# One chain of small operations for the norms of two token tiles

## The chip, the cores and the metric

One Trainium2 chip, one core of it. The metric is the device time of one execution in microseconds (us). The kernel before took 2983.17 us, the median of three runs (2980.04 to 2984.09). Each engine works through its own queue in order: PE (TensorE, products and transposes), PEld (loads of PE's stationary operand), DVE (VectorE), ACT (ScalarE), POOL (GpSimd) and SP (which issues the DMAs). An instruction that waits holds up all that stands behind it in its queue.

## The reference

Two layers over 512 latent and 256 context tokens of width 1024. A layer is a SwiGLU feed-forward (FFN1), a token mixing with three groups of heads (grouped-query attention, a long convolution, attention over compressed keys) and a second feed-forward (FFN2). Each of the three adds its gated result to the stream and norms the sum; before each stands a second norm with a scale and shift that depend on the conditioning:

```python
def layer_norm(x, g=None, b=None):
    xf = x.astype(jnp.float32)
    mu = jnp.mean(xf, -1, keepdims=True)
    var = jnp.mean(jnp.square(xf - mu), -1, keepdims=True)
    y = (xf - mu) * lax.rsqrt(var + EPS)
    ...
def rms_norm(x, g):
    xf = x.astype(jnp.float32)
    y = xf * lax.rsqrt(jnp.mean(jnp.square(xf), -1, keepdims=True) + EPS) * g
    ...
```

Inside the mixing, the query and key heads (width 64), the compressed queries (256) and the compressed keys (128) have the root-mean-square norm. So nearly everything that enters a product went through a reciprocal root just before.

## The kernel before

**Tiles.** Tokens lie on partitions in six tiles of 128: tiles 0 to 3 are latents, 4 and 5 context. `P[j]` is the stream of tile j. Each float32 factor is split into two float32r parts, and each product is three matmuls (`mm3`). `H` and `Hl` (in the rows Hhi, Hlo) hold the normed and modulated stream, transposed, for all tokens.

**The order.** All operations are first recorded. A list schedule (`Recorder.order`) then takes, for each engine, of what is ready the operation that stands first in the program; its table of costs and latencies sets the order in each queue, and so do the slots of the pools (22 units of 128x1024, 13 weight tiles, 12 small tiles, 8 PSUM banks): a tile takes a slot when an earlier one gives it back. All instructions are issued from line 295, so rows of the profile are told apart by tiles: p is PSUM, w a split weight, raw a weight as loaded, s a small tile, t a scratch unit, u a unit that lives longer.

**A norm.** `norm_stats` takes two `bn_stats` and one `bn_aggr` of a tile on DVE, adds EPS, makes the reciprocal root by `rsqrt` (a guess from the exponent's bits, then two polynomial steps; nine DVE operations of one column) and multiplies by minus the mean: 11 operations of one column for each tile. `norm` then applies it on ACT. `post` multiplies the sums by the gate (DVE), adds them to `P[j]` (POOL), norms `P[j]` and applies the gain on POOL and the bias on DVE. `pre` norms `P[j]` again, transposes it on PE, modulates it on ACT and writes H and Hl: PE starts the next stage with these transposes, and what they read (a scratch unit, t) is ACT's.

**The seams.** A feed-forward sums its 22 units of hidden columns in four parts. In the last one, `ffn` forms the down products of tiles 0, 1, 2 and 3 one after the other, each tile's two halves of 512 columns with six units in each (18 matmuls a half), and then of tiles 4 and 5 together, unit by unit in turns; after each tile come its `post` and the next stage's `pre`. `mix_out` does the same after the mixing with pairs of tiles, but with `post` and `pre` for each tile by itself. In the text a seam is the place where one stage's last sums end and the next one's first products begin: FFN1 to mixing at 606 to 683 us (layer 0) and 2203 to 2278 (layer 1), FFN2 to the next FFN1 at 1622 to 1690, mixing to FFN2 of layer 1 at 2577 to 2614.

**The mixing's norms.** `proj` multiplies H by a group of columns of the input weights, for one tile after the other, and calls `use` on each: `use_kv` norms two key heads (a chain of two columns) and the compressed keys (one column), `use_cq` the compressed queries (one column), `use_q` six query heads (six columns). The stretches 683 to 780 and 2278 to 2345 us hold most of this.

**Counts.** There are 82 chains of one column: 60 of layer norms and 22 of root-mean-square norms. There are also 12 of two columns for the key heads, 10 of six columns for the query heads, and three on pairs of input tiles at the start.

Of the kernel before, what the change touches and what calls it, by code (L numbers as in the profile page):

```python
# [24 lines left out]
SEQ = 512  # L25
# [24 lines left out]
class Recorder:  # L50
    """Takes down engine operations instead of issuing them, finds which must follow which, and issues them
    in the order of a list schedule: each engine takes, of what is ready, what stands first in the program.

    Tiles that share slots are handed them in program order, which keeps the schedule free of deadlocks.
    """

# [86 lines left out]
    def cost(eng, method, args, kw):  # L143
        """About how long (ns) the engine is held."""
# [34 lines left out]
    def order(self):  # L179
# [8 lines left out]
        # slots: the tiles of each tag in the order of their first use  # L188
# [9 lines left out]
        # a tile may take a slot before its turn where the program's order from there on still has its own  # L198
# [99 lines left out]
def weave(main, n, side, m):  # L298
    """Runs through both, main's n steps and side's m in proportion."""
    done = 0  # L300
    for i, _ in enumerate(main, 1):
        while done * n < i * m and done < m:
            next(side, None)
            done += 1
    for _ in side:
        pass


class _Slots:
    """The slots of a tag: when each falls free, and which tiles (by rank) have theirs."""  # L310
# [41 lines left out]
class Core:  # L352
    """The network's passes over one core's engines; tiles are 128 tokens, latents first."""
# [46 lines left out]
    def copy(self, out, in_):  # L400
        """A copy on whichever of the two engines is next in turn."""
# [7 lines left out]
    def weights(self, src, n, units=False):  # L409
        """Loads [128, n] of weights and splits them exactly into two float32r parts."""  # L410
# [9 lines left out]
    def mm3(self, out, sh, sl, mh, ml, first, last):  # L420
        """out (+)= s.T @ m with s = sh + sl, m = mh + ml."""
# [5 lines left out]
    def split(self, hi, lo, src, scale=None):  # L427
        """hi + lo = src (times a per-partition scale), both float32r; src may be in PSUM."""
# [9 lines left out]
    def rsqrt(self, y, v, t):  # L438
        """y = v ** -0.5 on small float32 tiles (t: scratch of the same shape)."""
        ts, tt = self.nc.vector.tensor_scalar, self.nc.vector.tensor_tensor  # L440
        stt = self.nc.vector.scalar_tensor_tensor
        one = v.shape[-1] == 1

        def vyy(t):
            if one:
                stt(t, v, y, y, ALU.mult, ALU.mult)
            else:
                tt(t, v, y, ALU.mult)
                tt(t, t, y, ALU.mult)

# [9 lines left out]
        if one:  # L460
            ts(p, p, t, 1.875, ALU.mult, ALU.add)
        else:
            tt(p, p, t, ALU.mult)
            ts(p, p, 1.875, None, ALU.add)
        tt(y, y, p, ALU.mult)

    def norm_stats(self, x):
        """(rstd, -mean * rstd, mean) of the rows of x [128, 1024]."""
        nc = self.nc
        st = self.small(24)  # L470
        for i, c in enumerate(HALVES):
            nc.vector.bn_stats(st[:, 6 * i:6 * i + 6], x[:, c])
        nc.vector.bn_aggr(st[:, 12:14], st[:, 0:12])
        r = self.small(4)
        nc.vector.tensor_scalar(r[:, 0:1], st[:, 13:14], EPS, None, ALU.add)
        self.rsqrt(r[:, 1:2], r[:, 0:1], r[:, 2:3])
        nc.vector.scalar_tensor_tensor(r[:, 3:4], st[:, 12:13], -1.0, r[:, 1:2], ALU.mult, ALU.mult)
        return r[:, 1:2], r[:, 3:4], st[:, 12:13]

# [1 line left out]
    def norm(self, x, out):  # L481
        """out = (x - mean) / deviation, row by row."""
        rstd, nmr, _ = self.norm_stats(x)
        for c in HALVES:
            self.nc.scalar.activation(out[:, c], x[:, c], AF.Identity, bias=nmr, scale=rstd)
        return out

    def norms(self, xs):
        """Norms the rows of several tiles in place, by one chain of small operations."""
# [14 lines left out]
        for j, x in enumerate(xs):  # L504
            for c in HALVES:
                nc.scalar.activation(x[:, c], x[:, c], AF.Identity, bias=nmr[:, j:j + 1], scale=y[:, j:j + 1])
        return xs

    def pre(self, l, j, x, kind):
        """H[:, :, tile j] = layer_norm(x) * (1 + scale) + shift."""  # L510
        nc = self.nc
        hn = self.norm(x, self.tmp())
        h = self.tmp()
        i = 0 if j < NLT else 1
        sh, sc = self.mcol[l][kind], self.mcol[l][kind + 1]
        for k0, c in zip((0, 4), HALVES):
            p = self.ps()
            for k in range(4):
                nc.tensor.transpose(p[:, 128 * k:128 * k + 128], hn[:, c][:, 128 * k:128 * k + 128], self.ident)
            for k in range(4):  # L520
                src, dst = p[:, 128 * k:128 * k + 128], h[:, c][:, 128 * k:128 * k + 128]
                b, m = sh[:, k0 + k, i:i + 1], sc[:, k0 + k, i:i + 1]
                nc.scalar.activation(dst, src, AF.Identity, bias=b, scale=m)
            hk = h[:, c].rearrange("p (k t) -> p k t", k=4)
            hi = self.H[:, k0:k0 + 4, 128 * j:128 * j + 128]
            nc.scalar.copy(hi, hk)
            nc.gpsimd.tensor_tensor(self.Hl[:, k0:k0 + 4, 128 * j:128 * j + 128], hk, hi.bitcast(F32), ALU.subtract)

    def post(self, j, P, acc, gate, gb, quick=False):
        """P = layer_norm(P + gate * acc, g, b); acc: pairs of a first column and the sums from there on."""  # L530
        nc = self.nc
        t = self.tmp()
        add = (nc.vector if quick else nc.gpsimd).tensor_tensor
        for c0, p in acc:
            c = slice(c0, c0 + p.shape[-1])
# [1058 lines left out]
```

## Time and profile before

| | |
|---|---|
| median of three runs | 2983.17 us |
| span of the profiled execution | 2980.4 us (no other time is given for that execution) |
| PE busy | 2850.9 us, 96% |
| DVE busy | 1781.7 us, 60% |
| ACT busy | 1057.1 us, 35% |
| POOL busy | 718.6 us, 24% |
| PE's idle time put down to ACT's scratch units t | 46.5 us in 26 waits |

A row of a stretch gives its length, then each engine's busy time (with the count of instructions), then PEclk, the mean clock that was granted to TensorE as a share of full speed. A row of the waits says what PE waited for: the engine and tile that came last, the us in total, how many times, and the longest. In rows of operations, out<-in are the tiles, then partitions x elements.

### The profile page before, as it was taken

Reading aid. Unit: us, or ns where it says so; the run is one execution under the profiler, and the core shown is the slowest. Engines: PE = TensorE matmul, PEld = TensorE weight load, DVE = VectorE, ACT = ScalarE, POOL = GpSimd, SP = SyncE. Lnnn points to the kernel's source line nnn. Section 1 sums busy time; section 2 is a strip of 40 time slices with the busy share of each in tenths; the row PEclk is TensorE's granted clock in tenths of the full one; section 3 lists DMA queues with packets and bytes.
Section 4 is the critical chain, followed back from the end, with each engine's and each line's share of the span. In section 5 each row is a group of like instructions: output and inputs, shape, how many; then the busy total and the mean of one; then the engine's idle time right before and its main releaser. Section 6 shows DMA issues by size and latency. Waiting matters only on the chain. (4 is left out here: it accounts for less than half of the span.)

```text
span 2980.4 us, 42000 instructions
## 1 busy us (share of the span) xinstructions
PE 2850.9 (96%) x16132; PEld 2431.1 (82%) x16132; DVE 1781.7 (60%) x4039; ACT 1057.1 (35%) x2050; POOL 718.6 (24%) x659
## 2 busy tenths in 40 slices
PE   7999999989999999999999999999998999899997
PEld 5888888868787789888887788888878777688886
DVE  6875757688667682757575744132268767723335
ACT  4212221255655653121222621211236647442221
POOL 2201223265011052013223410122145220310222
PEclk9999999989999999999999999999999999899999
DMA  7653434321021312434341231212122112123331
GB/s 262 230 159 117 138 124 137 110 100 52 30 70 39 107 44 71 148 121 150 109 149 46 96 119 57 78 51 70 71 84 71 41 50 93 57 92 106 99 107 56
DMA packets 105721, 291.42 MB, mean 98 GB/s; under 512 B 15184, under 2 KB 17392, under 8 KB 105520
## 3 DMA queue, kind: packets, MB, share of 16 engines
q1 hardware_dynamic: 105520, 288.73, 29.3%
q8 instruction: 127, 2.08, 0.3%
q14 instruction: 74, 0.61, 0.1%
HBM read 277.23 MB, written 11.45 MB: 97 GB/s over the span
## 5 line engine op out<-in xcount | busy, mean ns | idle before, releaser
L295 PE MATMUL p<-Hhi,w 128*128 128x256 f32 (+1 forms) x5536 | 1368.5, 337 | 8.0 <-DVE w L295 4.1
L295 PEld LDWEIGHTS p<-Hhi,w 128*128 128x128 f32 x5536 | 954.4, 191 | 121.9 <-DVE w L295 5.3
L295 PE MATMUL p<-Hlo,w 128*128 128x256 f32 (+1 forms) x2768 | 930.5, 337 | 0.0
L295 PE MATMUL p<-w,u 128*128 128x512 f32 x2904 | 671.6, 392 | 0.0
L295 DVE TENSOR_TENSOR w<-raw,w 128x1024 fp32r<-128x1024 f32 (+2 forms) x312 | 393.7, 1262 | 410.9 <-PE p L295 334.6
L295 PEld LDWEIGHTS p<-w,u 128*128 128x128 f32 x2904 | 546.1, 189 | 112.2
L295 ACT CAST w<-raw 128x1024 fp32r<-128x1024 f32 (+2 forms) x312 | 322.3, 1041 | 711.7 <-PE p L295 596.2
L295 PEld LDWEIGHTS p<-Hlo,w 128*128 128x128 f32 x2768 | 527.0, 190 | 54.5 <-POOL Hlo L295 1.2
L295 POOL TENSOR_TENSOR u<-t,u 128x512 fp32r<-128x512 f32 (+1 forms) x154 | 184.2, 1196 | 1246.2 <-ACT u L295 1170.8
L295 POOL TENSOR_TENSOR u<-u,t 128x512 f32<-128x512 f32 (+2 forms) x180 | 231.6, 1308 | 592.7 <-DVE t L295 367.1
L295 PE MATMUL p<-u,u 128*64 128x128 f32 (+7 forms) x2120 | 293.7, 326 | 22.2 <-DVE u L295 6.2
L295 DVE TENSOR_TENSOR t<-t,p 128x512 f32<-128x512 f32 (+1 forms) x160 | 90.6, 567 | 364.0 <-PE p L295 320.8
L295 PEld LDWEIGHTS p<-u,u 128*64 128x64 f32 (+4 forms) x2120 | 211.2, 160 | 84.0 <-issue 36.1
L295 DVE SCALAR_TENSOR_TENSOR junk<-adaw,crow 128x512 bf16<-128x512 f32 x256 | 201.4, 787 | 88.5 <-PE p L295 55.5
L295 ACT CAST u<-t 128x512 fp32r<-128x512 f32 (+1 forms) x154 | 81.3, 528 | 414.7 <-DVE t L295 407.2
L295 DVE SCALAR_TENSOR_TENSOR adaw<-adaw,crow 128x512 f32<-128x512 f32 x256 | 209.0, 816 | 6.1
L295 PE MATMUL p<-w,Hhi 128*128 128x416 f32 (+3 forms) x712 | 194.6, 356 | 7.9 <-DVE w L295 4.3
L295 DVE TENSOR_TENSOR t<-p,u 128x512 f32<-128x512 f32 x196 | 130.6, 684 | 100.3 <-PE p L295 99.5
L295 ACT ACTIVATE t<-p 128x512 f32<-128x512 f32 (+2 forms) x162 | 79.8, 496 | 273.8 <-PE p L295 273.7
L295 PE MATMUL p<-ident,t 128*128 128x128 f32 x848 | 124.8, 285 | 47.2 <-ACT t L295 42.2
L295 PEld LDWEIGHTS p<-ident,t 128*128 128x128 f32 x848 | 99.4, 145 | 69.9 <-ACT t L295 51.0
L295 PEld LDWEIGHTS p<-w,Hhi 128*128 128x128 f32 x712 | 131.2, 194 | 20.1 <-DVE w L295 9.0
(124 smaller groups left out, 2434.1 us busy)
## 6 DMA issues: line engine op xcount, KB each, us to landing
raw<-in_ffn_gu SPq DMA_DIRECT2D x176, 512.0 KB, 3.6
adaw<-in_ada_t SPq DMA_DIRECT2D x256, 256.0 KB, 2.8
raw<-in_ffn_down SPq DMA_DIRECT2D x88, 512.0 KB, 3.8
raw<-in_w_out_u SPq DMA_DIRECT2D x16, 512.0 KB, 3.3
u<-in_x_all SPq DMA_DIRECT2D x12, 512.0 KB, 7.6
xs<-u SPq DMA_DIRECT2D x12, 512.0 KB, 2.6
raw<-in_w_hy SPq DMA_DIRECT2D x12, 512.0 KB, 3.4
u<-grow SPq DMA_DIRECT2D x10, 512.0 KB, 5.1
```

Source lines behind the costliest of these rows:

```text
L295: getattr(getattr(self.nc, eng), method)(*args, **kw)
```

## The change

`rsqrt` is written in one way for any width, in ten operations. `stats` makes one chain of twelve for all tiles that it is given, each tile one column; `norms`, `pre` and `post` take lists of tiles. The last part of a feed-forward takes tiles in pairs (0, 1), (2, 3), (4, 5), each tile's two halves fully before the next tile's, then `post` and `pre` of both; the last feed-forward of all keeps single tiles (`step=1`). `mix_out` hands its pairs to `post` and `pre` as pairs. In the mixing, `proj` first takes the squares of a pair of tiles into one small tile (`take`) and then norms both (`use`): six columns for the key heads and compressed keys of two tiles, two for the compressed queries, twelve for the query heads. Comments are dropped, so line numbers stay. Built, the kernel has 606 fewer DVE instructions, 578 of them with a scalar operand and 28 TENSOR_TENSOR; the counts of PE, ACT, POOL and SP are the same.

```diff
     def rsqrt(self, y, v, t):
...
         ts(yi, yi, -1.0, 1595932665.0, ALU.mult, ALU.add)
-        vyy(t)
-        ts(t, t, -1.0, 2.38924456, ALU.mult, ALU.add)
-        stt(y, y, 0.703952253, t, ALU.mult, ALU.mult)
-        vyy(t)
+        tt(t, v, y, ALU.mult)
+        stt(t, t, -0.703952253, y, ALU.mult, ALU.mult)
+        stt(y, t, 1.68191409, y, ALU.add, ALU.mult)
+        tt(t, v, y, ALU.mult)
+        tt(t, t, y, ALU.mult)
         p = self.small(v.shape[-1])
         ts(p, t, 0.375, -1.25, ALU.mult, ALU.add)
-        if one:
-            ts(p, p, t, 1.875, ALU.mult, ALU.add)
-        else:
-            tt(p, p, t, ALU.mult)
-            ts(p, p, 1.875, None, ALU.add)
-        tt(y, y, p, ALU.mult)
...
+        tt(p, p, t, ALU.mult)
+        stt(y, p, 1.875, y, ALU.add, ALU.mult)
+
+    def stats(self, xs):
...
-    def post(self, j, P, acc, gate, gb, quick=False):
+    def post(self, Ps, accs, gates, gb, quick=False):
...
-        self.norm(P, P)
-        for c in HALVES:
-            nc.gpsimd.tensor_tensor(P[:, c], P[:, c], gb[0][:, c], ALU.mult)
-            nc.vector.tensor_tensor(P[:, c], P[:, c], gb[1][:, c], ALU.add)
+        self.norms(Ps)
+        for P in Ps:
+            for c in HALVES:
+                nc.gpsimd.tensor_tensor(P[:, c], P[:, c], gb[0][:, c], ALU.mult)
+                nc.vector.tensor_tensor(P[:, c], P[:, c], gb[1][:, c], ALU.add)
...
-                for js in [[j] for j in range(NLT)] + [[*range(NLT, ntok)]]:
-                    ps = {j: [] for j in js}
-                    for h in range(2):
-                        for j in js:
-                            ps[j].append((512 * h, self.ps()))
-                        for f in range(n):
-                            for j in js:
-                                down(ps[j][h][1], j, h, f)
+                for j0 in range(0, ntok, step):
+                    js = range(j0, j0 + step)
+                    ps = []
                     for j in js:
-                        self.post(j, P[j], ps[j], gate[j // NLT], gb, quick=j == tail)
-                        yield j
+                        ps.append([(512 * h, self.ps()) for h in range(2)])
+                        for h in range(2):
+                            for f in range(n):
+                                down(ps[-1][h][1], j, h, f)
+                    self.post([P[j] for j in js], ps, [gate[j // NLT] for j in js], gb, quick=j0 + step == tail)
+                    yield js
...
         def run(toks):
-            for j in toks:
+            toks = [*toks]
+            for q, j in enumerate(toks):
                 p = self.ps()[:, :n]
...
-                use(j, p)
+                take(j, p)
+                if (q + 1) % step == 0:
+                    use(toks[q + 1 - step:q + 1])
```

PE's queue before, at the end of FFN1 of layer 0 (row 3056 on): p_868 and p_869 are sums of tiles 4 and 5, t_822 is tile 0 after the norm of the mixing's `pre`.

```order
L295 MATMUL p_827<-ident_83,t_822 128x128 x4
L295 MATMUL p_869<-w_805,u_743 128x512
L295 MATMUL p_869<-w_806,u_743 128x512
L295 MATMUL p_869<-w_805,u_743 128x512
L295 MATMUL p_868<-w_805,u_743 128x512
L295 MATMUL p_828<-ident_83,t_822 128x128 x4
L295 MATMUL p_868<-w_806,u_743 128x512
```

The same place now (row 3072 on): p_866 is a sum of tile 5, t_827 and t_828 are tiles 0 and 1 after that norm.

```order
L295 MATMUL p_866<-w_799,u_707 128x512 x2
L295 MATMUL p_835<-ident_83,t_827 128x128 x4
L295 MATMUL p_866<-w_800,u_707 128x512
L295 MATMUL p_866<-w_799,u_707 128x512
L295 MATMUL p_838<-ident_83,t_828 128x128 x4
L295 MATMUL p_866<-w_805,u_743 128x512
L295 MATMUL p_836<-ident_83,t_827 128x128 x4
L295 MATMUL p_866<-w_806,u_743 128x512
L295 MATMUL p_839<-ident_83,t_828 128x128 x4
```

The transposes of tiles 0 and 1 have moved together, and from the interleaved sums of tiles 4 and 5 to those of tile 5, with tile 4's already behind them.

SP's queue before, at the same seam (row 281 on): xs_142 is the stream's copy in DRAM, u_283 and u_284 are tiles 0 and 1 of the stream, the raw tiles are the mixing's first weights.

```order
L295 DMA xs_142<-u_283 128x1024
L295 DMA adaw_2081<-in_ada_t 128x512
L295 DMA t_896<-in_ropeA 128x512
L295 DMA raw_933<-in_w_kv 128x832
L295 DMA xs_142<-u_284 128x1024
L295 DMA u_911<-in_hy_w 64x512
L295 DMA raw_936<-in_w_kv 128x832
L295 DMA raw_939<-in_w_kv 128x832
```

SP's queue now (row 283 on), with the same names for the stream.

```order
L295 DMA xs_142<-u_283 128x1024
L295 DMA xs_142<-u_284 128x1024
L295 DMA u_905<-in_hy_w 64x512
L295 DMA raw_927<-in_w_kv 128x832
L295 DMA u_906<-hdn 64x256
L295 DMA t_909<-in_hy_decay 128x256
L295 DMA raw_930<-in_w_kv 128x832
L295 DMA raw_933<-in_w_kv 128x832
```

The second of the four key and value weights was issued between the two stores; it now stands behind both.

## Rows read from the trace of the kernel before

**Rows 1.** Of the page's first part: busy us, share, instructions
```profile
PE 2850.9 (96%) x16132; PEld 2431.1 (82%) x16132; DVE 1781.7 (60%) x4039; ACT 1057.1 (35%) x2050; POOL 718.6 (24%) x659
```

**Rows 2.** Busy time by stretch; columns as the first line says
```profile
core 0: us, PE busy (x) PEld busy (x) DVE busy (x) ACT busy (x) POOL busy (x), PEclk, DMA share, GB/s
606.00:683.00 77.00, 62.33 (x317) 52.23 (x316) 63.14 (x175) 49.33 (x104) 47.80 (x37) 0.89 0.26 86
683.00:780.00 97.00, 84.27 (x504) 74.32 (x504) 81.96 (x362) 53.45 (x136) 32.72 (x72) 0.93 0.16 52
1622.00:1690.00 68.00, 57.80 (x346) 48.45 (x346) 58.62 (x161) 47.08 (x90) 38.26 (x29) 0.97 0.21 59
2203.00:2278.00 75.00, 64.24 (x346) 56.86 (x346) 68.82 (x209) 47.29 (x97) 49.94 (x56) 0.93 0.22 77
2278.00:2345.00 67.00, 58.41 (x289) 50.56 (x288) 57.79 (x235) 37.04 (x87) 30.41 (x49) 0.92 0.22 74
2577.00:2614.00 37.00, 23.06 (x142) 20.47 (x141) 32.51 (x95) 21.55 (x44) 18.24 (x13) 0.77 0.07 29
```

**Rows 3.** Waits of TensorE, 606 to 683: us in total, times, longest
```profile
PE p L295 <- ACT t L295: 10.3, 3, 6.4
PE p L295 <- DVE s L295: 3.1, 1, 3.1
```

**Rows 4.** Waits of TensorE, 683 to 780
```profile
PE p L295 <- DVE t L295: 4.0, 2, 2.0
PE p L295 <- DVE u L295: 2.4, 5, 0.9
```

**Rows 5.** Waits of TensorE, 1622 to 1690
```profile
PE p L295 <- ACT t L295: 10.2, 5, 3.5
```

**Rows 6.** Waits of TensorE, 2203 to 2278
```profile
PE p L295 <- ACT t L295: 6.9, 5, 4.2
```

**Rows 7.** Waits of TensorE, 2278 to 2345
```profile
PE p L295 <- DVE w L295: 4.1, 3, 3.3
```

**Rows 8.** Timeline of TensorE: start, us, operation, idle before it and its releaser
```profile
613.29 1.12 PE L295 MATMUL p<-ident,t 128*128 128x128 f32 x4 [6.35 <-ACT t L295]
```

**Rows 9.** VectorE's one-column operations: busy us, mean ns, idle before
```profile
L295 DVE SCALAR_TENSOR_TENSOR s<-s 128x1 f32<-128x1 f32 x180 | 70.4, 397 | 1.8
L295 DVE SCALAR_TENSOR_TENSOR s<-s,s 128x1 f32<-128x1 f32 x126 | 39.0, 317 | 0.8
L295 DVE TENSOR_SCALAR s<-s 128x1 f32<-128x1 f32 x246 | 34.0, 146 | 3.4 <-ACT t L295 1.5
L295 DVE TENSOR_TENSOR s<-s,s 128x1 f32<-128x1 f32 x82 | 24.5, 299 | 0.8
L295 DVE TENSOR_SCALAR s<-s 128x1 int32<-128x1 int32 x164 | 23.0, 146 | 1.2
L295 DVE TENSOR_SCALAR s<-s,s 128x1 f32<-128x1 f32 x82 | 16.7, 204 | 0.7
```

**Rows 10.** VectorE's two-column operations, same columns
```profile
L295 DVE TENSOR_TENSOR s<-s 128x2 f32<-128x2 f32 x108 | 16.7, 158 | 43.0 <-ACT t L295 42.0
L295 DVE TENSOR_TENSOR s<-s,s 128x2 f32<-128x2 f32 x78 | 15.5, 209 | 0.3
L295 DVE TENSOR_SCALAR s<-s 128x2 f32<-128x2 f32 x60 | 13.0, 227 | 0.3
L295 DVE SCALAR_TENSOR_TENSOR s<-s,s 128x2 f32<-128x2 f32 x15 | 2.5, 165 | 0.1
```

**Rows 11.** VectorE from 603 to 655 alone, same columns
```profile
L295 DVE SCALAR_TENSOR_TENSOR s<-s 128x1 f32<-128x1 f32 x24 | 10.2, 440 | 0.0
L295 DVE TENSOR_TENSOR w<-raw,w 128x832 fp32r<-128x832 f32 x4 | 4.1, 1014 | 2.0 <-PE p L295 2.0
L295 DVE TENSOR_SCALAR s<-s 128x1 f32<-128x1 f32 x24 | 3.2, 146 | 0.0
```

**Rows 12.** DMA issues: count, KB each, median us to landing
```profile
raw<-in_ffn_gu SPq DMA_DIRECT2D x176, 512.0 KB, 3.6
```

More of the change, by code (lines that the diff above doesn't have):

```diff
@@ L503, in norms @@
         nc.vector.scalar_tensor_tensor(nmr, mean, -1.0, y, ALU.mult, ALU.mult)
-        for j, x in enumerate(xs):
+        return [[x[:, j:j + 1] for x in (y, nmr, mean)] for j in range(n)]
+    def norms(self, xs, outs=None):
+        outs = outs or xs
+        for x, out, (rstd, nmr, _) in zip(xs, outs, self.stats(xs)):
             for c in HALVES:
-                nc.scalar.activation(x[:, c], x[:, c], AF.Identity, bias=nmr[:, j:j + 1], scale=y[:, j:j + 1])
-        return xs
-    def pre(self, l, j, x, kind):
+                self.nc.scalar.activation(out[:, c], x[:, c], AF.Identity, bias=nmr, scale=rstd)
+        return outs
@@ L511, in pre @@
+    def pre(self, l, js, xs, kind):
         nc = self.nc
-        hn = self.norm(x, self.tmp())
-        h = self.tmp()
-        i = 0 if j < NLT else 1
         sh, sc = self.mcol[l][kind], self.mcol[l][kind + 1]
[L516 to L527, printed above, removed]
@@ L529, in post @@
-    def post(self, j, P, acc, gate, gb, quick=False):
+        for j, hn in zip(js, self.norms(xs, [self.tmp() for _ in xs])):
+            h = self.tmp()
+            i = 0 if j < NLT else 1
+            for k0, c in zip((0, 4), HALVES):
+                p = self.ps()
+                for k in range(4):
+                    nc.tensor.transpose(p[:, 128 * k:128 * k + 128], hn[:, c][:, 128 * k:128 * k + 128], self.ident)
+                for k in range(4):
+                    src, dst = p[:, 128 * k:128 * k + 128], h[:, c][:, 128 * k:128 * k + 128]
+                    b, m = sh[:, k0 + k, i:i + 1], sc[:, k0 + k, i:i + 1]
+                    nc.scalar.activation(dst, src, AF.Identity, bias=b, scale=m)
+                hk = h[:, c].rearrange("p (k t) -> p k t", k=4)
+                hi = self.H[:, k0:k0 + 4, 128 * j:128 * j + 128]
+                nc.scalar.copy(hi, hk)
+                nc.gpsimd.tensor_tensor(self.Hl[:, k0:k0 + 4, 128 * j:128 * j + 128], hk, hi.bitcast(F32), ALU.subtract)
@@ L544, in post @@
[L544 to L547 removed]
+        for P, acc, gate in zip(Ps, accs, gates):
+            t = self.tmp()
+            for c0, p in acc:
+                c = slice(c0, c0 + p.shape[-1])
+                nc.vector.tensor_tensor(t[:, c], p, gate[:, c], ALU.mult)
+                add(P[:, c], P[:, c], t[:, c], ALU.add)
+        if quick:
+            for P, (rstd, _, mean) in zip(Ps, self.stats(Ps)):
+                for c in HALVES:
+                    nc.vector.scalar_tensor_tensor(P[:, c], P[:, c], mean, gb[0][:, c], ALU.subtract, ALU.mult)
+                    nc.vector.scalar_tensor_tensor(P[:, c], P[:, c], rstd, gb[1][:, c], ALU.mult, ALU.add)
+            return
@@ new lines, in mix, with take_kv @@
+        kvt, kvn = {}, {}
+        kvs = [None]
+        def take_kv(j, p):
+            t = kvt[j] = self.unit()
+            nc.scalar.copy(t[:, 512:928], p)
+            if j % 2 == 0:
+                kvs[0] = self.small(6)
+            i, p = j % 2, t[:, 512:928]
+            kn = kvn[j] = self.tmp()
+            self.head_squares(p[:, 0:128], 2, kvs[0][:, 2 * i:2 * i + 2])
+            nc.scalar.activation(kn[:, 256:384], p[:, 256:384], AF.Square, accum_out=kvs[0][:, 4 + i:5 + i])
+            nc.gpsimd.tensor_copy(Vj(j, 0, 128), p[:, 128:256])
@@ L1472, in run @@
             n = NLT if last else NT
-            for j, P in self.mix_out(l, n):
-                self.pre(l, j, P[j], 6)
+            for js, P in self.mix_out(l, n):
+                self.pre(l, js, [P[j] for j in js], 6)
             fill = (x for k in range(0, 0 if last else 6) for x in self.ada(l + 1, k))
-            for j in self.ffn(l, 2, n, P, fill, tail=n - 1 if last else None, first=FIRST[l]):
+            for js in self.ffn(l, 2, n, P, fill, tail=n if last else None, first=FIRST[l], step=1 if last else 2):
                 if last:
-                    for c in HALVES:
-                        self.load(self.out[128 * j:128 * j + 128, c], P[j][:, c])
+                    for j in js:
+                        for c in HALVES:
+                            self.load(self.out[128 * j:128 * j + 128, c], P[j][:, c])
                 else:
-                    self.pre(l + 1, j, P[j], 0)
+                    self.pre(l + 1, js, [P[j] for j in js], 0)
 @with_exitstack
```

180 lines of the change are left out of this document (78 added, 102 removed).

## The prediction, made before the changed kernel ran

> **What bounds the kernel now.** I read the page's busy shares first. PE works 2850.9 us of the 2980.4 us span, 96% [rows 1]: at most 129.5 us can be won without giving PE less work or a higher clock, and the change leaves PE's work as it is. So DVE's saving counts only where PE stands still and the last thing to come was behind DVE's chains.
>
> Next come the stretches [rows 2]. Idle time of PE is length less busy: 14.7 us in 606 to 683, 12.7 in 683 to 780, 10.2 in 1622 to 1690, 10.8 in 2203 to 2278, 8.6 in 2278 to 2345, 13.9 in 2577 to 2614; together 70.9, more than half of all idle time. DVE is busy 82 to 92% there, against 60% over the span [rows 1, 2].
>
> Then the waits of each stretch say what came last. In 606 to 683 it is ACT's scratch t (10.3 us) and a small tile of DVE (3.1) [rows 3]; in 683 to 780 DVE's t and u, 4.0 and 2.4 [rows 4]; in 1622 to 1690 t, 10.2 [rows 5]; in 2203 to 2278 t, 6.9 [rows 6]; in 2278 to 2345 a weight split on DVE, 4.1 [rows 7]. ACT's t is what `norm` writes, after the chain on DVE: ACT is named because it came last, yet it had room, 49.33 of 77 us [rows 2]. The clearest instance is at 613.29 us: the transposes of tile 0 waited 6.35 us for t [rows 8].
>
> **What the change takes from DVE.** A chain of one column costs 70.4 + 39.0 + 34.0 + 24.5 + 23.0 + 16.7 = 207.6 us over 82 chains, 2.53 us each (eleven operations for a layer norm) [rows 9]. A pair's chain has 4 TENSOR_SCALAR, 4 TENSOR_TENSOR and 4 SCALAR_TENSOR_TENSOR of two columns. By their rows it is 4 x 0.227 + 3 x 0.158 + 0.209 + 4 x 0.165 = 2.25 us [rows 10], for two tiles. Of the 60 layer norms by single tiles 56 become 28 pairs: 56 x 2.53 - 28 x 2.25 = 78.7 us less. These drop 56 x 11 - 28 x 12 = 280 instructions. The kernel loses 606; four last chains gain one each, so some 330 go with the mixing's norms. At the mean of the one-column rows, 207.6 us over 880 instructions or 0.236, they are 78 us. DVE goes from 1782 to about 1625 us, 9% less.
>
> No row shows an operation of twelve columns or one on a strided six. The bounds are 0.158 us (a TENSOR_TENSOR of two columns) and 0.397 (a SCALAR_TENSOR_TENSOR of one) [rows 9, 10]; I take the lower half, since a column more made nothing dearer than 0.227 there. The ends differ by 55 operations x 0.24 = 13 us of DVE, spread over two layers, and the range holds that.
>
> **What reaches PE, seam by seam.** Three things come into the way of a full gain. A pair's chain can't begin before the second tile's sums: tile 0 now waits 36 matmuls more, 36 x 62.33/317 = 7.1 us [rows 2]. Behind the waiting statistics stand, in DVE's queue, operations of the next pair, but the schedule puts ready work ahead of them. Second, the work that was next latest is still there: ACT, POOL and the weight splits, which share the queues. Third, what PE had as filler moves too. In 606 to 683 PE reaches the first transposes 25 matmuls later than before (4.9 us by the same pitch), between the sums of tile 5. All four sets stand together there, where tile 1's stood 30 matmuls behind tile 0's.
>
> Nothing in the rows tells how the wait divides between the chains and what is next. The bounds are nothing and all of the wait. I take half, and name what takes the other half.
>
> - 606 to 683: (10.3 + 3.1) / 2 = 6.7 us [rows 3]. Next late: the mixing's weight splits, 1.01 us each on DVE [rows 11], now issued together. The clock comes to this: the stretch had 0.89 of full clock, 1622 to 1690 with like work 0.97 [rows 2], so 0.08 x 77 = 6.2 us is lost to it. With half the stall gone I take half of that too, 3.1.
> - 683 to 780: (4.0 + 2.4) / 2 = 3.2 [rows 4]. Next late: POOL's rotary products, whose count is unchanged.
> - 1622 to 1690: 10.2 / 2 = 5.1 [rows 5]. Next late: ACT, busy 47.08 of 68 us [rows 2].
> - 2203 to 2278: 6.9 / 2 = 3.5 [rows 6]. Next late: POOL's low parts and the splits, as in layer 0.
> - 2278 to 2345: 4.1 / 2 = 2.1 [rows 7]. The split waits in DVE's queue among the small operations that go.
> - 2577 to 2614: nothing. The pair is ready about when tile 1 was, so tile 0 comes later and tile 1 no sooner; PE's 13.9 us idle and its 0.77 of clock [rows 2] stay. All or a third of it either way are the bounds, -4.6 to +4.6.
> - The end: four single chains with one operation more, 0.165 to 0.227 us each [rows 10], of which the last tile's counts: +0.3 us with its issue.
> - The other norms of `mix_out` in layer 0 and the pairs at the start lie beside products that run on; ±1.
>
> Sum: 6.7 + 3.1 + 3.2 + 5.1 + 3.5 + 2.1 - 0.3 = 23.4 us. The profiled span becomes 2980.4 - 23.4 = 2957.0. The median of the runs shown is 2.8 us above that span, so the time is 2959.8, say 2960 us.
>
> **A rule against it.** In 603 to 655 us a SCALAR_TENSOR_TENSOR of one column takes 440 ns in the mean of 24, a TENSOR_SCALAR of one column 146 [rows 11]; over the span the first takes 397 [rows 9]. The operations that read two tensors are the dear ones while POOL works. A single chain has five such of eleven, a pair's chain eight of twelve. If the two-column rows were cheap only because they stand where POOL is quiet, a pair's chain at a seam costs 8 x 0.440 + 4 x 0.227 = 4.4 us, and two single ones 2 x (5 x 0.440 + 6 x 0.146) = 6.2: 1.8 us saved and not 5.06 - 2.25 = 2.8. [...]
>
> A second rule speaks against pairing as such. The Trainium skill, "Perfetto Trace Analysis", section "Optimizing Scalar/DVE Operations", says that grouping amortizes a fixed cost where the engine is saturated, and that where an engine isn't but causes bubbles elsewhere, breaking instructions up may end work sooner. At 82 to 92% busy in the seams [rows 2] DVE is nearer to the first case; the second case is the rival *nothing* below.
>
> **The rivals.**
> - *More.* The chains are all of the wait, since DVE is over 80% busy wherever PE stands: 13.4 + 6.2 + 6.4 + 10.2 + 6.9 + 4.1 = 47.2 us, less 0.3. Time 2980.4 - 46.9 + 2.8 = 2936 us. For it: a seam holds twelve layer-norm chains, and 12 x 2.53 - 6 x 2.25 = 16.9 us of DVE's queue goes there, more than any of these waits. Against: ACT and POOL each work 47 to 49 us of the 77 in the first seam [rows 2], and theirs doesn't shrink. Chance 0.13.
> - *The dear two-input operations.* The gain without the clock, 20.6 us, times 1.8/2.8 is 13.2, less 0.3: 2980.4 - 12.9 + 2.8 = 2970 us. Chance 0.15.
> - *Nothing.* The pair's wait for its second tile, 7.1 us, eats what the shorter chain gives, and transposes come as late as before: about 2983 us, give or take 4. For it: the first set of transposes can't come sooner than the second tile. Against: two sets come with it, and PE has the sums of two more tiles and more before it needs them. Chance 0.12.
> - *Slower: the weights of the next stage.* The down weights give their slots back when tile 5 has used them. Before, tiles 4 and 5 ran unit by unit, and the first weight was done with 60 matmuls before the end of the sums, 11.8 us; now it is with 30, 5.9 us. The second key and value weight moved behind the stores of both tiles in SP's queue. A weight takes 3.6 us to land [rows 12] and four splits take 4 x 1.014 = 4.1 us [rows 11], together 7.7. It decides from the point where the slots come later than 7.7 us before PE needs the weights; 5.9 is past it by 1.8, but PE has transposes and filter products first. If PE stood the full 7.7 us at each of the three seams with this loop, and the gains there were lost, the time is 2980.4 + 23.1 - 3.2 - 2.1 + 0.3 + 2.8 = 3001 us; from 2989 on for half of it. Chance 0.10.
>
> That the chains would not be paired is excluded by the order and the count of instructions.
>
> **How the numbers follow.** The forecast has 0.50, with its own range of 2947 to 2973 (the halves taken as a quarter or three quarters of the waits, ±10, and the bounds of the small places). The range leaves 0.08 below it, half of *more*, and 0.10 above, most of *slower*: 2936 to 2986 us. A difference under 0.2%, 6 us, can't be told from none. Faster than 2977: the forecast, *more* and three quarters of *dear*, 0.74. Within 6 us: *nothing* and the rest of *dear*, 0.16. Slower than 2989: 0.10.
>
> **What would show it.** DVE's busy time near 1625 us, its two-column operations at 0.16 to 0.23 us each. If those read 0.4 in the seams, the dear case holds. PE's waits for t at 606 to 683, 1622 to 1690 and 2203 to 2278 halved, from 27.4 to about 14 us. The clock of the first of these above 0.92. Waits of PE for w that appear after the last sums, above 5 us in all, would show the weights' case. Unchanged waits for t with a DVE that has idle time would show that the second tile's sums set the time. The prediction is wrong if PE's idle time in the six stretches stays within 6 us of 70.9.

## The result: 1.4% slower

The changed kernel took 3024.58 us (median of four, 3021.92 to 3026.60) beside 2982.81 for the kernel before; the ratio is 1.0142 with a 95% interval of 1.0129 to 1.0155. The forecast was 2960, the range ended at 2986. The profiled execution has a span of 3024.8 us, 44.4 more than before.

The engines' row of the page after, against [rows 1]:

```profile
PE 2869.9 (95%) x16132; PEld 2451.6 (81%) x16132; DVE 1707.2 (56%) x3433; ACT 1054.7 (35%) x2050; POOL 718.0 (24%) x659
```

DVE did lose 606 instructions and 74.5 us of work, and PE got later. PE's busy time is 19.0 us longer for the same 16132 instructions, so of the 44.4 us PE stood idle for 25.4 more (154.9 against 129.5) and took 19.0 longer over its own work. By the clock records of the two traces 124.9 us of that work ran at the lower level of the clock (half of full speed, 1.2 GHz), 76.7 before. The same stretches of work as in [rows 2], shifted by what had been lost before each (columns as there; the third is new and is followed by its counterpart of the kernel before):

```profile
609.00:688.00 79.00, 60.27 (x289) 50.83 (x288) 51.67 (x118) 43.87 (x90) 39.56 (x32) 0.83 0.24 84
688.00:785.00 97.00, 87.27 (x545) 78.28 (x544) 69.04 (x197) 58.39 (x152) 40.70 (x78) 0.95 0.16 52
1062.00:1187.00 125.00, 115.15 (x738) 105.84 (x736) 92.66 (x206) 61.02 (x112) 47.81 (x35) 0.95 0.30 98
1640.00:1725.00 85.00, 67.46 (x363) 55.14 (x361) 77.05 (x186) 44.12 (x87) 40.32 (x29) 0.86 0.28 87
2239.00:2316.00 77.00, 61.28 (x334) 55.23 (x332) 53.72 (x131) 39.76 (x82) 48.68 (x60) 0.93 0.25 88
2620.00:2659.00 39.00, 23.79 (x151) 22.29 (x150) 24.64 (x63) 17.84 (x35) 15.77 (x11) 0.78 0.08 28
```
```profile
1055.00:1170.00 115.00, 111.42 (x734) 102.47 (x733) 65.66 (x169) 60.15 (x111) 44.86 (x34) 0.99 0.21 69
```

PE's idle time rose from 14.7 to 18.7 us in the first seam, from 3.6 to 9.9 behind the first mixing, from 10.2 to 17.5 between FFN2 and FFN1, from 10.8 to 15.7 in the next seam. In the six stretches of [rows 2] together (2278 to 2345 is now 2316 to 2382) it is 85.5 us, from 70.9. DVE, meanwhile, is less busy in the first seam, 51.67 us of 79 against 63.14 of 77. The waits, in 609 to 688:

```profile
PE p L295 <- ACT t L295: 12.6, 5, 6.4
PE p L295 <- DVE w L295: 5.8, 2, 5.4
```

in 1640 to 1725:

```profile
PE p L295 <- ACT t L295: 9.2, 3, 7.7
PE p L295 <- DVE w L295: 4.8, 2, 2.8
```

and in 2239 to 2316:

```profile
PE p L295 <- DVE w L295: 8.6, 2, 6.3
PE p L295 <- ACT t L295: 5.8, 2, 4.7
```

The waits for t come to 27.6 us in these three seams; in [rows 3], [rows 5] and [rows 6] they were 27.4. They did not shrink at all, and the waits for weights rose to 19.2 us. In the kernel before there were 2.1, in the first and the third of these seams:

```profile
PE p L295 <- DVE w L295: 0.6, 2, 0.4
PE p L295 <- DVE w L295: 1.5, 1, 1.5
```

The granted clock fell to 0.83 in the first seam (0.89 before) and to 0.86 between FFN2 and FFN1 (0.97); in the third seam it stayed at 0.93.

All programs give PE the same number of instructions, so the n-th can be compared in time. The lag of a run behind the kernel before, taken at a few times of that kernel, gives the loss of each stretch; a column's head is the time at which its stretch ends. This table is worked out from the traces of single executions. Runs whose programs are the same up to a column differ there by up to 3.7 us (e1 and e8, or the changed kernel and e5, up to 585) and by some 2 us later, so smaller steps are not told apart from noise. Stretches are in us of the kernel before, and the runs are explained below.

```
                    0-585  -810 -1055 -1170 -1615 -1750 -2192 -2360 -2560 -2650  -end   sum
changed              3.3    1.5   2.5   9.3   1.0  16.9   1.5   2.3   4.1   2.5  -0.6  44.4
e1 mixing norms      5.9   -6.3   2.5  -0.7   0.0   0.0   0.9  -8.7   3.3   0.7  -0.6  -3.0
e2 layer norms       5.6    1.8   0.2  10.2   1.0  17.7   1.5   9.4   0.5   2.5  -0.5  49.8
e3 4, 5 in turns     6.0    8.1   2.7   9.3   1.0  17.4   1.5   1.3   5.0   2.5  -0.6  54.3
e4 ada held          3.3    3.9   2.5  11.1   0.0   5.5   0.0   3.0   4.3   2.7  -0.5  35.7
e5 mix_out single    6.5   -0.7   0.4  -0.3   0.0  17.1   1.5   1.8   4.5  -0.1  -0.6  30.1
e7 single chains     3.2    0.0   2.6  -2.0   0.5  10.1   1.0  -2.7   1.7   2.3  -0.6  16.0
e8 single tiles      2.2   -4.2   2.5   0.3   0.0  12.7   1.0  -9.6   3.8  -0.5  -0.6   7.8
e9 e8, ada held      4.7   -3.3   2.8   0.4   0.0   6.5   0.0  -8.2   3.2   0.9  -0.6   6.4
e13 tied             4.4    1.5   0.8   0.3   1.0  10.5   1.0   2.6   8.2   2.5  -0.5  32.3
e14 untied           3.1   -3.8   2.5  -1.4   0.5  10.7   1.0  -3.6   1.4   2.3  -0.5  12.3
```

The largest loss, 16.9 us, lies between FFN2 and FFN1: 8.6 us of it are idle time and 8.3 a longer busy time of PE, at a clock of 0.90 (0.99 before). There PE waited 7.66 us for the context tiles:

```profile
1717.35 3.04 PE L295 MATMUL p<-ident,t 128*128 128x128 f32 x13 [7.66 <-ACT t L295]
```

DVE was busy, but with something else. Its groups from 1677 to 1718 (busy us, mean ns):

```profile
L295 DVE SCALAR_TENSOR_TENSOR junk<-adaw,crow 128x512 bf16<-128x512 f32 x16 | 14.3, 896 | 0.2 <-DMA adaw<-in_ada_t 0.2
L295 DVE SCALAR_TENSOR_TENSOR adaw<-adaw,crow 128x512 f32<-128x512 f32 x15 | 12.9, 861 | 0.2
```

31 sums for the conditioning (ada, a matrix by vector product along rows, wanted only later) fill 27 of these 41 us. In the kernel before none of them begins between 1615 and 1750 us. The list schedule takes what is ready, so it probably put them here because by its own table DVE had nothing else to do while it waited for a pair; its times were not read out.

### The profile page after: what moved, and what is told of

Same layout as the page of the kernel before. It is cut to its first block, busy times and chain, and to the rows that moved or that the text cites. A ratio compares the mean times of both kernels' runs of the same rounds, so it can differ in the third digit from the quotient of the medians.

```text
span 3024.8 us, 41357 instructions
## 1 busy us (share of the span) xinstructions
PE 2869.9 (95%) x16132; PEld 2451.6 (81%) x16132; DVE 1707.2 (56%) x3433; ACT 1054.7 (35%) x2050; POOL 718.0 (24%) x659
## 4 chain that ended last, share of the span: by engine, by line
PE 58%; DVE 8%; ACT 2%; issue 1%; POOL 1%; DVEq 0%; ACTq 0%; POOLq 0%
PE p L295 58%; DVE s L295 3%; DVE u L295 2%; ACT t L295 2%; DVE t L295 1%; DVE w L295 1%; POOL u L295 1%; ACT u L295 0%; POOL Hlo L295 0%; DVE adaw L295 0%; DVE junk L295 0%; ACT Hhi L295 0%; POOL t L295 0%; DVE Hlo L295 0%; ACT w L295 0%
## 5 line engine op out<-in xcount | busy, mean ns | idle before, releaser
L295 PE MATMUL p<-Hhi,w 128*128 128x256 f32 (+1 forms) x5536 | 1375.8, 339 | 16.9 <-ACT Hhi L295 10.0
L295 PEld LDWEIGHTS p<-Hhi,w 128*128 128x128 f32 x5536 | 962.1, 192 | 130.7 <-ACT Hhi L295 10.5
L295 DVE SCALAR_TENSOR_TENSOR junk<-adaw,crow 128x512 bf16<-128x512 f32 x256 | 212.9, 832 | 64.7 <-PE p L295 36.7
L295 PEld LDWEIGHTS p<-w,Hhi 128*128 128x128 f32 x712 | 132.7, 197 | 28.9 <-DVE w L295 15.8
```

The source lines that it names most:

```text
L295: getattr(getattr(self.nc, eng), method)(*args, **kw)
```

## The experiments

Four theories. *Tie*: with one chain for two tiles the first tile's norm cannot begin before the second tile's sums and statistics, so all that follows comes late and in a burst. *Weights*: tile 4 whole ahead of tile 5 gives weight slots back later. *Ada*: the schedule fills DVE's gaps with conditioning sums. *Operations*: the chain's own two-column operations are dear beside POOL.

**e1, e2: halves of the change.** The new root with either the mixing's norms in pairs or the layer norms in pairs (the last feed-forward part with them):

```diff
 e1: rms, proj, take_*, use_* of the changed kernel; norm_stats, norm, pre, post, ffn, mix_out of before
 e2: stats, norms, pre, post, ffn, mix_out of the changed kernel; rms, proj, use_* of before
```

> The kernel before with the new root and the paired norms of the mixing alone; the layer norms and the last feed-forward part stay by single tiles. If the 42 us are lost where layer norms end a stage, this is near before: 2975 to 2992 us. If pairing as such (waiting for the second tile, two-column operations beside POOL) is what costs, the mixing's q and kv stretches lose too and it is above 3000 us.

> The other half: new root, paired layer norms and the last part by pairs; the mixing's norms as before. Seams as the cause: 3015 to 3032 us. If the loss were in the mixing's norms: 2975 to 2992 us.

Measured: e1 2976.42 us, ratio 0.9976 (0.9967 to 0.9986); e2 3032.23, ratio 1.0167 (1.0152 to 1.0182). The mixing's pairs gain 6.4 us: the table has -6.3 and -8.7 in the q and kv stretches, and less in sum, though its 5.9 at the start is not told apart from the 2.2 that e8 has there with the same program. The layer norms' half loses 49, at the upper end of what was expected. The two add up to the whole.

**e3: tiles 4 and 5 in turns again.**

```diff
...
+                    if j0 == NLT:
+                        ps = [[(512 * h, self.ps()) for h in range(2)] for j in js]
+                        for h in range(2):
+                            for f in range(n):
+                                for j in js:
+                                    down(ps[j - j0][h][1], j, h, f)
...
```

> The changed kernel, but tiles 4 and 5 take the last part's units in turns again, half by half, as before; norms stay paired. Theory of the late weight slots (first weights done 60 matmuls before the end, not 30): PE's waits for w in the seams (5.8, 4.8 and 8.6 us) go, 3003 to 3014 us. Theory of the conditioning sums (ada) drawn into the seams, or of the pair's own wait: within 5 us of 3024.

Measured 3033.88, ratio 1.0173 (1.0158 to 1.0188): slower still, and outside what either theory expected. The first split of the mixing's weights on DVE moved from 643.21 to 622.27 us (619.20 before), so the slots did come earlier, but PE then waited 2.13 us for the second one and 4.67 for the third, 6.8 in all (5.8 in the changed kernel). Undoing this alone gives nothing back.

**e4: the conditioning sums held.** In the recorder alone, each DVE operation on an adaw tile of the next feed-forward counts as needing the last norm of the stage ahead of it:

```diff
+        if self.hold is not None and eng == "vector" and any(str(t).startswith("adaw") for t in tiles):
+            deps.add(self.hold)
...
+            self.nc.hold = max(i for i, op in enumerate(self.nc.ops) if op[0] == "vector")
...
```

> The changed kernel, but in the recorder's order no conditioning sum (ada) of a feed-forward may stand before the last norm of the stage ahead of it; every instruction is kept. Theory that these sums, some 32 of 0.7 to 1.8 us on DVE, hold up the context pair's norm in FFN2 to FFN1: the 18.4 us lost there go, and part of the 10.6 lost behind the first mixing: 2995 to 3010 us. Theory of the weight slots: within 5 us of 3024.

Measured 3017.08, ratio 1.0116 (1.0101 to 1.0131): outside what either theory expected. FFN2 to FFN1 lost 5.5 us in place of 16.9, so ada is most of that place. PE's idle time there is back at that of the kernel before (9.5 us against 10.3 from 1615 to 1750); what is left is a longer busy time (131.1 against 124.8 us, at a clock of 0.94 against 0.99). The loss behind the first mixing stayed (11.1).

**e5: `mix_out` by single tiles.**

```diff
-                    self.post([P[j] for j in js], [[(512, acc[j])] for j in js], [gt, gt], gb)
-                    yield js, P
+                    for j in js:
+                        self.post([P[j]], [[(512, acc[j])]], [gt], gb)
+                        yield (j,), P
```

> The changed kernel, but the output projection hands post and pre each tile by itself, as before. Theory that a tile which waits for its pair's second one delays what comes after: the 9.3 us lost from 1055 to 1170 and the 2.5 from 2560 to 2650 go, 3009 to 3016 us, and nothing else moves. Theory of the chains' two-column operations: within 4 us of 3024.

Measured 3013.09, ratio 1.0109 (1.0094 to 1.0124), as expected: 9.3 and 2.5 us are gone at those two places, and nothing else moved by more than the noise of the table. What happened there is seen on ACT, in the changed kernel:

```profile
1106.82 2.93 ACT L295 ACTIVATE t<-u,s 128x512 f32<-128x512 f32 x4 [14.00 <-DVE s L295]
1116.69 0.88 ACT L295 ACTIVATE u<-u,s 128x512 f32<-128x512 f32 x1
1132.52 2.93 ACT L295 ACTIVATE t<-u,s 128x512 f32<-128x512 f32 x4
```

and in the kernel before:

```profile
1088.30 1.52 ACT L295 ACTIVATE t<-u,s 128x512 f32<-128x512 f32 x2 [5.64 <-DVE s L295]
1100.25 0.85 ACT L295 ACTIVATE u<-u,s 128x512 f32<-128x512 f32 x1
```

ACT stood 14.00 us for the pair's chain, then had the norms of tiles 2 and 3 and their modulation at once, and the first norm of the context pair (u<-u,s) waited behind them until 1116.69, though its chain was done at 1108.5. The second norm began at 1132.52, and PE waited 2.6 and 1.4 us for the two parts of H at 1141 and 1143. With 5.9 for t these are the 9.9 us of idle time in the stretch (3.6 before); the remaining 3.0 of the 9.3 us are a longer busy time of PE (clock 0.95 against 0.99).

**e6, e12: the operations.** e6 puts the two columns two elements apart; e12 issues each TENSOR_SCALAR of the pair once for each column.

```diff
 e6:
-        r = self.small(4 * n)
-        v, y, t, nmr = [r[:, n * i:n * i + n] for i in range(4)]
+        r = self.small(10 * n).rearrange("p (k j i) -> p k i j", k=5, i=2)
+        v, y, t, nmr, q = [r[:, i, 0] for i in range(5)]
 e12:
+            for c in range(w) if w == 2 else [slice(0, w)]:
+                c = slice(c, c + 1) if w == 2 else c
+                self.nc.vector.tensor_scalar(out[:, c], x[:, c], *a)
```

> The changed kernel, but the layer-norm chains' two columns lie two elements apart. One-column TENSOR_SCALAR took at most 215 ns beside POOL in the kernel before, two adjacent columns up to 1291 now. If adjacency makes the two-column ones wait for POOL, they stay under 250 ns here, DVE's chains shorten, and 3 to 12 us come back: 3012 to 3021 us. If it is the width or nothing of the kind: within 3 us of 3024.

> The changed kernel with the chain shared, but each TENSOR_SCALAR of the pair issued once for each column, so none reads two columns; DVE has some 100 instructions more. 41 two-column ones beside POOL took 478 ns in the mean, one-column ones 146 to 154. If their wait for POOL costs PE: 3008 to 3018 us. If what costs is that the chain begins with the second tile and nothing overlaps it: 3021 to 3032.

Measured 3023.77 and 3026.08 (ratios 1.0146 and 1.0147), each as its second theory expected: neither helps. The dear operations are real, though. In the changed kernel from 636.9 us, while POOL ran four products in a row (second fence), four steps of one chain took about 1.2 us each (the second and third of three TENSOR_SCALAR that last 2.71 together, then the TENSOR_TENSOR and one of the two SCALAR_TENSOR_TENSOR), and the split that PE waited for stood behind them:

```profile
636.89 2.71 DVE L295 TENSOR_SCALAR s<-s 128x2 f32<-128x2 f32 x3
639.63 1.18 DVE L295 TENSOR_TENSOR s<-s 128x2 f32<-128x2 f32 x1
640.85 1.38 DVE L295 SCALAR_TENSOR_TENSOR s<-s 128x2 f32<-128x2 f32 x2
643.21 1.02 DVE L295 TENSOR_TENSOR w<-raw,w 128x832 fp32r<-128x832 f32 x1
```
```profile
637.07 4.95 POOL L295 TENSOR_TENSOR u<-u,u 128x512 f32<-128x512 f32 x4
```

Over the runs, the integer TENSOR_SCALAR of the chain (mean ns) in the changed kernel, in e6 and in e12:

```profile
L295 DVE TENSOR_SCALAR s<-s 128x2 int32<-128x2 int32 x72 | 20.7, 289 | 0.9
```
```profile
L295 DVE TENSOR_SCALAR s<-s 128x2 int32<-128x2 int32 x72 | 20.7, 289 | 0.9
```
```profile
L295 DVE TENSOR_SCALAR s<-s 128x1 int32<-128x1 int32 x152 | 19.0, 144 | 0.2
```

So distance makes no difference, one column does, and the time doesn't follow. The other eight operations of the chain read two tensors and stay as long as they were (the two-column TENSOR_TENSOR at 205 ns in e12, 214 in the changed kernel; SCALAR_TENSOR_TENSOR at 260 in both).

**e7, e8, e9, e11: chains and tiles undone step by step.** e7 keeps the pair's order but gives each tile a chain of its own; e8 goes back to single tiles everywhere in the layer norms (tile 4 still whole ahead of tile 5); e9 and e11 are e8 and e7 with ada held between FFN2 and FFN1.

```diff
 e7:
+        return [self.stat(x)[0] for x in xs]
...
 e8, with the edit of e5:
-            for js in self.ffn(l, 2, n, P, fill, tail=n if last else None, first=FIRST[l], step=1 if last else 2):
+            for js in self.ffn(l, 2, n, P, fill, tail=n if last else None, first=FIRST[l], step=1):
...
```

> The changed kernel with its order by pairs, but each tile has a chain of its own in the layer norms (twelve operations of one column). If the shared chain is what costs (its operations in a row, beside POOL): near the mixing norms' kernel, 2976 to 2995 us. If the order by pairs costs (post of both, then pre of both, and the sums of 4 and 5): 3010 to 3035 us, since DVE has some 330 instructions more.

> The changed kernel with single tiles in post, pre and chains everywhere; from the changed last part only tile 4 whole ahead of tile 5 stays, and the mixing's pairs. If pairing is the whole loss: 2972 to 2985 us. If tile 4 ahead of tile 5 (late weight slots) costs: 5 to 15 us more, 2985 to 2995, in the three seams with that loop.

> The kernel with single tiles in the layer norms (2991 us), and no conditioning sum of the next feed-forward ahead of the last norm between FFN2 and FFN1. If the 12.7 us that it still lost there come from these sums: 2974 to 2982 us. If they come from tile 4's sums standing whole ahead of tile 5's (weights late): 2987 to 2994.

> Pair order with single chains (3000.6 us), and the conditioning sums held at the seam from FFN2 to FFN1 as in the run before. If the sums cause the 10.1 us lost there: 2988 to 2995 us. If the pair order does: 2997 to 3003.

Measured: e7 3000.57, between the two expectations; e8 2991.29, as its second theory expected, though in one seam and not in three; e9 2985.05 (2982.56 to 2989.27), also between; e11 2997.78, a small effect (-2.8), as its second theory expected. From these and e1 the 42 us divide: 3024.6 to 3000.6 (24.0) for the shared chain; to 2991.3 (9.3) for the order by pairs; to 2976.4 (14.9) for tile 4 ahead of tile 5, nearly all of it at FFN2 to FFN1, where 6.2 of it is ada (e9 against e8); and 6.4 the other way for the mixing's pairs. What costs the 6.5 us that e9 still loses there was not separated: PE waits 0.3 us for w in it, its idle time is 2.0 us longer than before and its busy time 4.5. The order of undoing matters, as e3 shows: with pairs in place, tiles 4 and 5 in turns gave nothing.

**e13, e14: the tie by itself.** Two chains of one column, in the pair's order; in e13 both are recorded as needing the statistics of the second tile, so they stand behind them in DVE's queue.

```diff
+        nc.tie = len(nc.ops) - 1
...
+        if self.tie is not None and eng == "vector":
+            deps.add(self.tie)
```

> Pair order with a chain of one column for each tile, but in DVE's queue both chains stand behind the statistics of the pair's second tile, as a shared chain must. If the tie to the second tile is what cost the 24 us between 3024.6 and 3000.6: 3018 to 3035 us. If the shared chain's own operations cost them (two columns, twelve steps in a row): 2996 to 3006.

> The same code without the tie: each chain may start with its own tile's statistics. The counterpart of the run above; by both theories near the single chains in pair order, 2996 to 3006 us.

Measured: tied 3011.51 (ratio 1.0097, 1.0080 to 1.0114), between the two expectations; untied 2995.71 (1.0047, 1.0032 to 1.0062), just under what was expected. The tie alone costs 15.8 us, mostly in the seams up to 810 and 2360 and behind the latter. It is the larger part of the 28.9 us between the changed kernel and e14, not all of it.

**e15, e16: what of the other 13 us.** In the changed kernel the schedule puts larger operations between the steps of a chain, since it takes a step's result to be ready 130 ns later. Here, small DVE operations count as ready at once, so that a chain stands in a row; e16 is the same rule in e1.

```diff
...
-                lat = 0.0 if e == f == "tensor" else ...
+                lat = 0.0 if e == f == "tensor" or e == f == "vector" and ops[n][6] < 210.0 else ...
```

> The changed kernel, every instruction kept, but in the recorder's order a small DVE operation counts as ready at once after the small one before it (it assumed 130 ns), so a chain's twelve steps stand in a row in DVE's queue; before, 116 other operations (weight splits of 1.2 us, conditioning sums of 0.7 us) stood between the steps of 18 chains. If what the tie leaves open (3011.5 for tied single chains against 3024.6) is these operations between the steps: 3003 to 3015 us. If it is the two columns' own time: within 4 us of 3024.

> The same rule in the faster kernel (mixing norms in pairs, layer norms by single tiles, 2976 us), as a candidate to beat both. There two chains fill each other's gaps already, so a chain in a row helps the first tile and delays the second: 2968 to 2982 us.

Measured 3036.58 (1.0177) and 3044.64 (1.0205), both far above what any theory expected, so the theory falls. e16 is 68 us slower than e1 with the same instructions. The rule moves other engines' work as well as the chains, so this is not the price of a chain in a row.

What the other 13 us are can be read from the kept traces. PE's row in e13:

```profile
PE 2856.6 (95%) x16132; PEld 2441.7 (81%) x16132; DVE 1736.0 (58%) x3805; ACT 1056.1 (35%) x2050; POOL 717.8 (24%) x659
```

Its span is 3012.7 us, so PE stood idle for 156.1 us, as long as in the changed kernel (154.9), but its own work took 13.3 us less: 98.8 us of it ran at the lower level of the clock, against 124.9. Two places have most of the difference, behind the first mixing (0.3 us lost against 9.3, where the changed kernel has the burst on ACT) and FFN2 to FFN1 (10.5 against 16.9). What in the changed kernel's order brings the lower clock stays open.

**e10: the mixing's pairs with the old root.** All of before but the mixing's norms.

> The kernel before with the mixing's norms in pairs, and the root as before. All kernels with the new root lost 2 to 6 us before 130 us, where the three pairs of inputs are normed. If the root or the order it brings does that: 2968 to 2974 us, below the 2976 of the mixing norms with the new root. If not: 2973 to 2980.

Measured 2977.52, ratio 0.9980 (0.9970 to 0.9989): no different from e1, as expected if the root costs nothing. The root is not what costs at the start: e10 lags by 3.1 us at 585 us though its program up to 679 us is that of the kernel before. e1 and e10 are the versions that beat both kernels.

## Why the prediction was wrong, step by step

*That DVE's chains are what PE waits for*: the reading of the waits was right as far as it went, but not its use. A wait for t ends with the norm's arrival, which depends on when the chain begins, on its length and on ACT. The step that failed is "I take half": it counted the shorter work as an earlier end. Half of 13.4, 10.2 and 6.9 us was to go in the three seams; the waits for t among them, 27.4 us, became 27.6, and the idle time of the six stretches rose by 14.6 us.

*The clock* was to give 3.1 us back in the first seam. It fell there from 0.89 to 0.83, and over the whole kernel PE took 19.0 us longer for the same instructions. The text has no term for a loss of this kind, neither in its sum nor in its rivals.

*The price of a chain* was mis-sized. I took durations for occupancy. In the kernel before, several chains stand interleaved on DVE, and a step starts some 0.06 to 0.13 us after the one ahead of it, though each lasts 0.14 to 0.21:

```profile
1087.27 0.17 DVE L295 SCALAR_TENSOR_TENSOR s<-s 128x1 f32<-128x1 f32 x1
1087.35 0.27 DVE L295 TENSOR_SCALAR s<-s 128x1 int32<-128x1 int32 x3
1087.54 0.21 DVE L295 SCALAR_TENSOR_TENSOR s<-s 128x1 f32<-128x1 f32 x1
1087.67 0.21 DVE L295 TENSOR_SCALAR s<-s,s 128x1 f32<-128x1 f32 x1
1087.79 0.21 DVE L295 TENSOR_SCALAR s<-s 128x1 f32<-128x1 f32 x2
1087.91 0.15 DVE L295 TENSOR_TENSOR s<-s,s 128x1 f32<-128x1 f32 x1
```

A lone pair's chain in the changed kernel has 0.19 us from step to step, since each needs the one before:

```profile
1643.79 0.57 DVE L295 TENSOR_SCALAR s<-s 128x2 f32<-128x2 f32 x3
1644.40 0.16 DVE L295 TENSOR_TENSOR s<-s 128x2 f32<-128x2 f32 x1
1644.59 0.36 DVE L295 SCALAR_TENSOR_TENSOR s<-s 128x2 f32<-128x2 f32 x2
1644.98 0.36 DVE L295 TENSOR_TENSOR s<-s 128x2 f32<-128x2 f32 x2
```

Twelve of these are 2.3 us, as forecast for a pair, but two interleaved chains of eleven at about 0.09, as at this quiet place, are 2.0, not 5.06. Over the whole trace the chains' small operations (TENSOR_SCALAR, TENSOR_TENSOR and SCALAR_TENSOR_TENSOR on small tiles) went from 1308 to 702 and lost 147.8 us of summed durations, near the 157 of the text; but the time in which no other DVE operation ran beside them fell by only 90.2, since they overlap one another and larger operations. With 15.7 us more of other work DVE's total fell by 74.5. e14, with 372 instructions more than the changed kernel and 57 us more of DVE, is 29 us faster: of the two cases in the prediction's second rule it was the second, in which breaking up ends work sooner.

*The pair's wait for its second tile*, 7.1 us, was named, and left out of the sum as if the half covered it; it is the larger part of the shared chain's loss (15.8 us, e13 against e14). The sign that the text gave for it, waits for t unchanged with DVE idle, is what the profile shows in the first seam and the third (DVE busy 51.67 of 79 us and 53.72 of 77); between FFN2 and FFN1 the conditioning sums filled DVE. The sign of the weights' case, waits for w above 5 us, was there too.

*The first mixing's output* I set at ±1, "beside products that run on". It lost 9.3 us, and PE waited there for t and for the context pair's H. This place was not read at all.

*The conditioning sums* did not appear in the text. The order shows them, drawn into the seam before the context pair's norm; e4 and e9 put 11.4 and 6.2 us on them.

*The weights' rival* has the waits for w, 19.2 us, for it, and tile 4 whole ahead of tile 5 does cost 14.9 us with single tiles (e8 against e1). That late weights are what costs there isn't shown: in e8 PE waits 3.7 us for w at FFN2 to FFN1, in e9 0.3, and e9 still loses 6.5. e3 says that it isn't the first thing to undo. Of the rivals, *slower* was the case, with 0.10, at 3001 for the wrong main reason; *nothing* had the mechanism of the largest single part and the wrong price.

*The mixing's norms* went the way that was forecast: 5.3 us was put on them, and e1 is 6.4 faster than the kernel before. That the size agrees is partly luck. DVE lost 25.4 us by them (e10), not 78, and the waits are not where most of the gain lies. The stretch from 585 to 810 us in the kernel before, and the same instructions of PE in e1:

```profile
585.00:810.00 225.00, 197.60 (x1133) 169.63 (x1132) 183.95 (x631) 120.32 (x284) 92.02 (x117) 0.93 0.20 65
```
```profile
590.90:809.60 218.70, 191.40 (x1133) 165.37 (x1132) 174.48 (x469) 119.68 (x283) 94.01 (x117) 0.96 0.21 69
```

The waits for DVE's t and u fell from 6.4 to 4.0 us, but others grew: PE's idle time is 27.3 us (27.4 before). The 6.2 us are busy time, at a clock of 0.96 (0.93 before). That the pairs cost nothing here because the second tile follows within one projection, while PE has other tiles' products, is argued and not shown.

*The dear two-input operations.* In [rows 11] the operations with two inputs were the dear ones, 440 ns against 146. But the rival priced the two-column TENSOR_SCALAR, of one input, at 0.227 us beside POOL too, and in the changed kernel it took up to 1.29 us there. The Trainium skill, "SBUF — State Buffer", section "Who interferes with whom", says that a DVE instruction with at most one SBUF input does not contend with GpSimd outside the 2-port modes, and that `tensor_scalar` can enter those when its operands meet their conditions. The trace agrees with both halves, 216 ns at most on one column and up to 1291 on two; whether the two columns ran in such a mode no run here shows. The kernel before had it already: of its 24 two-column TENSOR_SCALAR begun while POOL was busy, 5 took over 400 ns, up to 1226, and the mean of 0.227 hid them. Taking it away (e12) gave nothing back. (The rival's saving of 1.8 us a pair is 1.7 without rounding.)

## What to carry to other kernels

A norm that serves two tiles waits for the later one: merge chains where the second tile follows at once and the engine behind has other work, not at the seam where the first tile opens the next stage. Price small dependent operations by the step from start to start in their own surroundings, not by their durations; interleaved chains already hide each other. Count a change in PE's stalls twice, as waiting and as the clock at which its next work runs: here 25.4 and 19.0 us. When a list schedule sees a gap it fills it, so look in the new order for what has moved in ahead of the work that PE waits for.

## What the runs showed of the hardware

A TENSOR_SCALAR on one column, with constants or with another column as its scalar, took at most 216 ns whether POOL worked or not (492 in the kernel before, 198 of them begun while POOL was busy). On two columns beside POOL, 16 of 41 in the changed kernel took over 400 ns, up to 1291; away from POOL all 109 stayed under 171. Columns two elements apart gave the same (16 of 41, up to 1294). Why one column is spared, these runs do not tell.

The same 16132 matmuls and transposes kept PE busy for 2850.9 us in the kernel before and for 2869.9 in the changed one, 76.7 and 124.9 us of them at the lower level of the clock.

Twelve dependent steps on DVE were not better off with nothing between them: the order that put them in a row cost 12 us with 28 pair chains (e15) and 68 us with single ones (e16). How much of that is DVE standing between the steps, and how much the work that then came elsewhere, was not separated.
